# Seven products instead of eight for the pooling branch's first projection, with the weight sums made by GpSimd

## The chip, the cores and the metric

The kernel runs on one core of one Trainium2 chip. The metric is the device time of one execution in microseconds (us), and a kernel's time is the median of its runs. The engines are named as the profile names them: PE is TensorE, PEld its weight loads, DVE is VectorE, ACT is ScalarE, POOL is GpSimd and SP is SyncE, which here only issues DMAs.

## The reference

One layer of a hybrid encoder over 2048 positions of width 1024, in float32. The part that matters here:

```python
xn = rmsnorm(x, norm1_g[l])
z = xn @ w_in[l]
u_pool, zq, zf, zi, zo, zg = jnp.split(z, splits, axis=-1)
gates = jax.nn.sigmoid(zg + b_gate[l]).reshape(B, S, N_BRANCHES, D_MODEL)
ya = pool_mixer(u_pool, pool_w[l], pool_scale[l]) @ w_pa[l]
yb = hgrn2_mixer(zq, zf, zi, zo, lower_bounds[l], hgrn_norm_g[l]) @ w_pb[l]
merged = gates[:, :, 0] * ya + gates[:, :, 1] * yb
x = x + merged @ w_o[l]
x = x + conv_glu_ffn(rmsnorm(x, norm2_g[l]), w_up[l], conv_w[l], conv_b[l], w_down[l])
```

`pool_mixer` gives 512 channels, `w_pa` is 512 x 1024. The change concerns the product with `w_pa` alone.

## The kernel before

The sequence is worked in two halves of 1024 positions. Each half has two row blocks of 512 positions, called hf = 0 and 1 in the code. A half runs through these stages, one after another on PE: the projection `io`; 14 units of the input projection (named fr, gr and ur in the profile, for forget/query, gates and pooling input); `pa`, the projection of the pooled rows with `w_pa`; `pb`, the same for the HGRN branch; the output projection `wo`; the up-projection `up` and the down-projection `dn` of the feed-forward network.

Every float32 product is made of three matmuls: each operand is split into a high half (a cast on ACT, line 231 for weights and line 655 for rows) and a low half (a subtraction on DVE, lines 232 and 656), and high x high, high x low and low x high are added up in PSUM. All matmuls of the projections are issued on line 148.

All projections but `pa` and `pb` use a scheme with seven products instead of eight for a 2 x 2 block product (Winograd's form of Strassen's). A `Unit` holds two blocks of output channels for both row blocks. Its seven products, P1 to P7, come in the order P1, P6, P5, P7, P2, P4, P3 and take as their row operand the forms B11, T2, T1, T3, B21, T4 and B22; T1 to T4 are sums and differences of row blocks, and four of the seven weights are sums of weight blocks, s1 to s4. Three PSUM banks of a unit, X, Z and V, collect the products, and after most products DVE or ACT takes an intermediate result out. In the first half the weight sums of the input projection are made by POOL (line 443), partly in place in the raw weight tiles, and kept in DRAM for the second half.

`pa` and `pb` are plain. `branch` goes through eight tiles of 128 output channels in `M_ORDER`; for each tile and each row block a chain of 4 x 3 matmuls of 128x512 fills one bank, and one DVE instruction multiplies it by its gate (lines 1516 and 1518, output `ya` in pa). The gates come back from DRAM as tiles `gl`, asked for three channel tiles ahead.

Weights go through one `Stream` in the order of use: SP loads raw tiles (line 197) into a ring of 8, ACT and DVE split them into a ring of 6 `ops` tiles, and at most `LOOKAHEAD` = 4 tiles are made ahead of the one in use. Most other SBUF tiles come from one ring of 77 slots of 512 columns.

Side work runs in generator tasks, which are advanced one step after every six matmuls. Four of them matter here. `pa_task` starts with the last gate unit's first product, fetches the eight pooled tiles (`mx`, four for each row block, written to DRAM before by the pooling tasks) and splits them (`mxs`). Three runners carry the HGRN heads; the last of them end during pa. `halves_task` fetches and splits the HGRN outputs (`oT`, split to `oTs`) for pb; it starts in pa with the fifth of eight channel tiles (`O_AT`). `prepare` makes sums of later weights by DMA and pauses from the last gate unit to the end of pb. The order on each engine is set by a scheduler from the program's order and a time model, with a few dependencies written by hand.

Of the kernel before, what the change touches and what calls it, by code (L numbers as in the profile page):

```python
# [15 lines left out]
ALU = mybir.AluOpType  # L16
# [65 lines left out]
def tile_trunk(  # L82
# [26 lines left out]
    def slot(name, cols=TB, dt=F32):  # L109
        return slots.tile([P, cols], dt, tag="s", name=name, padded_shape=[P, 528])  # L110
# [32 lines left out]
    def join(task):  # L143
        while task.live:
            task.step()

    def mm(*args, **kw):
        count[1] = pe.matmul(*args, **kw)  # L148
        count[0] += 1
        if count[0] % MM_PER_TICK == 0:  # L150
            tick()
# [193 lines left out]
    def plan_one(key, src):  # L345
        r = stream.raw(src)
        stream.op(key, lambda nm, r=r: r.tile, [r])
# [44 lines left out]
    def plan_unit(key, src, kind, i, order, b0):  # L392
        mv, mg = proj_tiles(kind, i)
        if b0:
            unit = sums_of_unit(src, mv, mg, lambda p: lambda: kept["in", (kind, i), SUM_OF[p]])
        else:
            unit = weights_of_unit(src[mv], src[mg], (kind, i))
        for p in order:
            fn, raws = unit[p]()
            stream.op(key, fn, raws)  # L400

    def plan_mixer(b0):
        plan_io(b0)
        for kind, i in PROJ:
            if (kind, i) == ("u", 0):
                plan_one("pw", pool_wt)
            plan_unit("in", w_in_t, kind, i, ORDER, b0)
        for key, src in (("pa", w_pa_t), ("pb", w_pb_t)):
            for i in range(8):
                plan_one(key, src[i // 2][:, i % 2 * 512 : i % 2 * 512 + 512])  # L410
        plan_rows("wo", w_o, R_OUT, KD // 2)

    def proj_tiles(kind, i):
# [6 lines left out]
    def quarters(src_v, src_g):  # L420
        return [s[:, c * 512 : (c + 1) * 512] for s in (src_v, src_g) for c in range(2)]
# [8 lines left out]

        return {p: (lambda p=p: plan(p)) for p in ORDER}

    def weights_of_unit(src_v, src_g, unit):
        src = quarters(src_v, src_g)
        raws, made = {}, {}

        def raw(i):
            if i not in raws:
                raws[i] = stream.raw(src[i])
            return raws[i]  # L440

        def comb(key, t, x0, x1):
            pool.tensor_tensor(t, x0, x1, ALU.add)  # L443
            made[key] = t
            return t

        def plan(p):
            rs = [raw(i) for i in {"P1": (0,), "P6": (0, 2, 3), "P5": (2,), "P7": (0,),
                                   "P2": (1,), "P4": (3,), "P3": (1,)}[p]]

            def fn(nm):
                if p == "P6":
                    q0, q2, q3 = (r.tile for r in rs)
                    comb("s3", q0, q0, q2)
                    comb("s2", slot(f"{nm}s2"), q0, q3)
# [6 lines left out]
                keep(("in", unit, SUM_OF[p]), t)  # L462
                return t

            return fn, rs

        return {p: (lambda p=p: plan(p)) for p in ORDER}
# [181 lines left out]
    def split(src, name, on_pool=False):  # L649
        hi = slot(name + "h", TB, F32R)  # L650
        lo = slot(name + "l", TB, F32R)
        if on_pool:
            up = pool.tensor_scalar(hi, src, 1.0, 0.0, ALU.mult, ALU.add)
        else:
            up = act.copy(hi, src)
# [302 lines left out]
    def fetch(d, name, eng=sp):  # L958
        t = slot(name)
        eng.dma_start(t, d)  # L960
        return t
# [189 lines left out]
    def value(dst, a, ps):  # L1151
        if a is None:
            act.copy(dst, ps)
            return
        t, how = a
        if how == "from":
            return dve.tensor_tensor(dst, ps, t, ALU.subtract)  # L1157
        return dve.tensor_tensor(dst, t, ps, ALU.add if how == "add" else ALU.subtract)  # L1158

    class Unit:  # L1160
# [9 lines left out]

        def multiply(self, p, forms, late):
            xs = need(forms, FORM[p], late)
            self.forms = forms
            w = stream.get(self.key)
# [5 lines left out]
            for k in range(4):  # L1180
# [6 lines left out]
                mm(ps, wl, xh, start=False, stop=k == 3, skip_group_check=True)  # L1187
            stream.used(1)

        def after(self, p):  # L1190
            bk, t = self.bank, self.t
# [174 lines left out]
    def mixer(b0, forms, late):  # L1366
# [93 lines left out]
        def gate(s, m, hf):  # L1460
            if (s, m, hf) not in gates:
                gates[s, m, hf] = fetch(gd[s, m, hf], f"gl{b0 + hf}_{s}_{m}")
            return gates[s, m, hf]

        def pa_task():
            yield from halves_task(md, range(4), mixed, "mx", 2)
            for m in M_ORDER[:2]:
                for hf in range(2):
                    gate(0, m, hf)

        emits = {"fq": emit_fq, "u": emit_u, "g": emit_g}
        mixed, oT = {}, {}
# [41 lines left out]
        def gated(t, hf, g, ps):  # L1514
            if hf:
                dve.scalar_tensor_tensor(t, g, -1.0, ps, ALU.mult, ALU.mult)
            else:
                dve.tensor_tensor(t, g, ps, ALU.mult)

        def evac_a(m, hf, g, ps):  # L1520
            y[m, hf] = slot(f"ya{b0 + hf}_{m}")
            gated(y[m, hf], hf, g, ps)

        def evac_b(m, hf, g, ps):
            gated(g, hf, g, ps)
# [3 lines left out]
                two = {(h, r): y[k + r * (KD // 2), h] for h in range(2) for r in range(2)}  # L1529
                add_forms(two, yf, k, f"yf{b0}", eng=dve)  # L1530

        join(mtask)
        otask = []

        def start_o(n):
            if n == O_AT:
                otask.append(Task(halves_task(od, range(HEADS), oT, "oT", O_LAG)))

        branch("pa", 0, mixed, evac_a, start_o)
        while any(t.live for t in runners):  # L1540
            for t in runners:
                if t.live:
# [334 lines left out]
```

## Time and profile before

| | |
|---|---|
| median of 3 runs | 2521.32 us (2520.7 to 2521.7) |
| profiled execution | 2522.21 us |
| its span, first to last instruction | 2520.5 us |
| mean granted clock of TensorE | 0.998 |
| PE busy | 2506.8 us, 99% |
| DVE busy | 1943.3 us, 77% |
| ACT busy | 1196.0 us, 47% |
| POOL busy | 747.0 us, 30% |
| pa's matmuls, share of the chain that ended last | 4% |

The profile is that of one execution. Times within it count from its first instruction. In a row of a view that groups instructions, the line, engine, operation, output and inputs come first, then the count, the busy time in us, the mean of one instruction in ns, and the idle time of the engine just before with what ended it. A row of the view by stretches gives for each engine its busy time and instructions, then the granted clock, the DMA engines' busy share and GB/s.

### The profile page before, as it was taken

What the parts mean: (1) busy time and instruction counts of PE and PEld (TensorE: products, weight loads), DVE (VectorE), ACT (ScalarE), POOL (GpSimd) and SP (SyncE); (2) the same over time, 40 slices, a digit from 0 to 9 for tenths busy, and PEclk for the clock granted to TensorE, in tenths of its full rate; (3) what the DMA queues carried; (4) which work ended last, traced back from release to release, by engine and by line L of the source; (5) the groups of instructions that cost most, each with busy time, mean ns of one, the idle gap of its engine ahead of it and who ended that gap; (6) DMA issues with size and microseconds to landing.
All of it is one profiled execution on the core that took longest, in us unless ns stands there. A gap on an engine that the chain in (4) does not pass through costs nothing.

```text
span 2520.5 us, 35649 instructions
## 1 busy us (share of the span) xinstructions
PE 2506.8 (99%) x11508; PEld 2055.4 (82%) x11508; DVE 1943.3 (77%) x3476; ACT 1196.0 (47%) x2250; POOL 747.0 (30%) x1127
## 2 busy tenths in 40 slices
PE   9999999999999999999999999999999999999998
PEld 7888888888888888888788888888888888888887
DVE  7788877597998778885596778766979887778755
ACT  6534444235555445553554444442355555445534
POOL 4343452003344333551320202100033433325410
PEclk9999999999999999999999999999999999999999
DMA  8877787777888789897345343457344454447852
GB/s 271 271 201 223 212 218 226 251 204 244 207 253 240 223 224 246 265 364 233 114 155 155 105 134 109 142 158 236 124 155 120 153 150 138 149 135 247 319 165 98
DMA packets 252332, 493.76 MB, mean 196 GB/s; under 512 B 26544, under 2 KB 43056, under 8 KB 251824
## 3 DMA queue, kind: packets, MB, share of 16 engines
q1 hardware_dynamic: 184512, 313.60, 39.6%
q0 software_dynamic: 42656, 112.74, 17.6%
q10 hardware_dynamic: 24976, 65.13, 7.6%
q8 instruction: 91, 1.49, 0.3%
q14 instruction: 97, 0.79, 0.1%
HBM read 381.79 MB, written 187.17 MB: 226 GB/s over the span
## 4 chain that ended last, share of the span: by engine, by line
PE 98%; ACT 1%; POOL 0%; DVE 0%; DMA 0%; issue 0%; SPq 0%; POOLq 0%; DVEq 0%; ACTq 0%
PE dn_P L148 16%; PE up_Z L148 15%; PE up_X L148 10%; PE up_V L148 10%; PE wo_P L148 6%; PE gr_Z L148 5%; PE gr_V L148 4%; PE gr_X L148 4%; PE pa L148 4%; PE pb L148 4%; PE io_Z L148 3%; PE fr_Z L148 3%; PE fr_X L148 2%; PE io_V L148 2%; PE fr_V L148 2%; PE pl L1025 2%
## 5 line engine op out<-in xcount | busy, mean ns | idle before, releaser
L231 ACT CAST ops<-raw 128x512 fp32r<-128x512 f32 x786 | 485.4, 620 | 852.3 <-PE dn_P L148 180.2
L232 DVE TENSOR_TENSOR ops<-raw,ops 128x512 fp32r<-128x512 f32 x786 | 578.3, 738 | 226.1 <-ACT ops L231 219.8
L1613 DVE SCALAR_TENSOR_TENSOR e<-h,cols,e 128x512 f32<-128x512 f32 x176 | 143.1, 817 | 31.3 <-ACT e L1611 26.4
L1611 ACT ACTIVATE e<-h,cols 128x512 f32<-128x512 f32 x176 | 142.3, 815 | 25.0 <-DVE h L1158 18.3
L1616 DVE SCALAR_TENSOR_TENSOR e<-h,cols,e 128x512 f32<-128x512 f32 x176 | 133.9, 770 | 2.5
L960 POOL DMA_DIRECT2D g_P<-dg_P x154 | 84.0, 546 | 161.0 <-PE dn_P L148 110.8
L1268 POOL TENSOR_TENSOR gf_P<-e,e 128x512 f32<-128x512 f32 x44 | 61.1, 1390 | 149.6 <-DVE e L1622 96.1
L1268 POOL TENSOR_TENSOR gf_P<-gf_P,e 128x512 f32<-128x512 f32 x44 | 59.3, 1348 | 72.1 <-DVE e L1622 71.6
L1606 POOL COPY h<-h 128x2 f32<-128x2 f32 x88 | 40.2, 468 | 117.5 <-DVE h L1157 110.6
L1620 ACT ACTIVATE e<-e 128x512 f32<-128x512 f32 x88 | 55.6, 632 | 38.7 <-DVE e L1616 38.6
L1408 POOL TENSOR_TENSOR q<-q,qs 128x512 f32<-128x512 f32 x16 | 21.4, 1335 | 168.0 <-ACT qs L1407 168.0
L1608 POOL COPY hist<-h 128x2 f32<-128x2 f32 x88 | 35.5, 404 | 118.5 <-DVE h L1158 116.7
L443 POOL TENSOR_TENSOR raw<-raw,raw 128x512 f32<-128x512 f32 x28 | 38.9, 1390 | 102.0 <-DVE ops L232 101.0
L1158 DVE TENSOR_TENSOR h<-up_u,up_V 128x512 f32<-128x512 f32 x88 | 60.0, 682 | 10.3 <-PE up_V L148 9.9
L1243 DVE TENSOR_TENSOR x<-x,wo_P 128x512 f32<-128x512 f32 x88 | 56.0, 680 | 12.1 <-PE wo_P L148 11.9
L1445 ACT ACTIVATE gt<-gt,cols 128x512 f32<-128x512 f32 x48 | 34.8, 725 | 59.4 <-DVE gt L1158 42.5
L1243 DVE TENSOR_TENSOR ac<-ac,dn_P 128x512 f32<-128x512 f32 x72 | 47.0, 680 | 16.7 <-PE dn_P L148 16.6
L1010 POOL COPY qm<-q 128x64 f32<-128x64 f32 x64 | 27.1, 447 | 99.1 <-DVE q L1042 19.6
L1636 POOL DMA_DIRECT2D dg_P<-gf_P x88 | 50.8, 577 | 8.1 <-POOL gf_P L1268 7.4
L1193 ACT COPY up_e<-up_X 128x512 f32<-128x512 f32 x44 | 25.8, 587 | 57.7 <-PE up_X L148 52.6
L1606 POOL COPY h<-hist 128x2 f32<-128x2 f32 x88 | 45.0, 519 | 27.4 <-DVE m_T42l L656 27.4
L1025 PE MATMUL pl<-qm,k 128*128 128x192 f32 x256 | 50.2, 325 | 0.0
(1202 smaller groups left out, 8019.9 us busy)
## 6 DMA issues: line engine op xcount, KB each, us to landing
g_P<-dg_P POOLq DMA_DIRECT2D x154, 256.0 KB, 6.2
raw<-in_w_up_t SPq DMA_DIRECT2D x132, 256.0 KB, 3.3
raw<-in_w_in_t SPq DMA_DIRECT2D x98, 256.0 KB, 3.5
dg_P<-gf_P POOLq DMA_DIRECT2D x88, 256.0 KB, 4.0
dg_P<-e SPq DMA_DIRECT2D x66, 256.0 KB, 3.6
raw<-in_w_dn SPq DMA_DIRECT2D x66, 256.0 KB, 3.8
x<-in_x SPq DMA_DIRECT2D x64, 256.0 KB, 4.9
gd<-gt ACTq DMA_DIRECT2D x64, 256.0 KB, 3.5
```

Source lines behind the costliest of these rows:

```text
L148: count[1] = pe.matmul(*args, **kw)
L231: self.mark = act.copy(hi, v)
L232: low = self.low = dve.tensor_tensor(lo, v, f32(hi), ALU.subtract)
L960: eng.dma_start(t, d)
L1025: ins = pe.matmul(pa_[:, c * 192 : c * 192 + 192], ks[:, (i + c) * P : (i + c + 1) * P], mv[:, c].rearrange("p s x -> p (s x)"), start=Tru ...
L1158: return dve.tensor_tensor(dst, t, ps, ALU.add if how == "add" else ALU.subtract)
L1243: dve.tensor_tensor(t, t, ps[j], ALU.add if sg > 0 else ALU.subtract)
L1268: pin(eng.tensor_tensor(t, x0, x1, op))
L1606: pool.tensor_copy(h[:, 0:2], hist[:, mt] if hf == 0 else hs[s, 0][:, TB : TB + 2])
L1611: in_turn(act.activation(t, h[:, 2:], AF.Identity, bias=col(o_cb + mt), scale=col(o_cw + 4 * MF + mt)))
L1613: in_turn(second(dve.scalar_tensor_tensor(t, h[:, 1 : 1 + TB], col(o_cw + 2 * MF + mt), t, ALU.mult, ALU.add)))
L1616: dve.scalar_tensor_tensor(t, h[:, 0:TB], col(o_cw + mt), t, ALU.mult, ALU.add)
```

## The change

`pa` takes the form with seven products. The 1024 output channels are handled in two groups (d = 0, 1). A group has two `Unit`s (e = 0, 1), each with two channel tiles, i and i + 4. A weight tile of 512 columns now holds, for one product, two blocks of 128 rows for both units, so a product is 2 units x 2 x 3 matmuls, and there are 14 weight tiles instead of 8. Each group loads four raw quarters; POOL makes the sums s1 to s4 of them, s1, s3 and s4 in place in the raw tiles, s2 in a slot. Unlike those of the input projection they are not kept, and are made again in the second half.

`pa_task` fetches the same eight tiles, all before the first form, and makes the seven forms of two tiles each: t1, t2 and t4 on DVE, t3 on POOL, the negated B22 on ACT, and 14 splits. `emit_a` takes the results out: for block (0, 0) DVE multiplies PSUM by the gate; for the other three DVE combines PSUM with an intermediate result and POOL multiplies by the gate. Gates are asked for two products ahead of their use. The task for `oT` starts before the third product of the second group. The task of the forms need no longer be finished before pa starts; each product waits for its own form.

```diff
+        for d in range(2):
+            unit = weights_of_unit([w_pa_t[d][:, c * 512 : c * 512 + 512] for c in range(4)])
+            for p in ORDER:
+                fn, raws = unit[p]()
+                stream.op("pa", fn, raws)
+        for i in range(8):
+            plan_one("pb", w_pb_t[i // 2][:, i % 2 * 512 : i % 2 * 512 + 512])
...
         def pa_task():
-            yield from halves_task(md, range(4), mixed, "mx", 2)
-            for m in M_ORDER[:2]:
-                for hf in range(2):
-                    gate(0, m, hf)
+            t = {}
+            for hf, g in ((0, 0), (0, 1), (1, 0), (1, 2), (1, 1), (1, 3), (0, 2), (0, 3)):
+                while (b0 + hf, g) not in md:
+                    yield 1
+                t[hf, g] = fetch(md[b0 + hf, g], f"mx{b0 + hf}_{g}")
...
+            for j in range(2):
+                form("B11", j, t[0, j])
+                yield 1
+            t1, t2 = [], []
+            for j in range(2):
+                t1.append(minus("t1", j, t[1, j], t[0, j]))
+                t2.append(minus("t2", j, t[1, j + 2], t1[j]))
+                form("T2", j, t2[j])
+                yield 1
+            t3 = [minus("t3", j, t[1, j], t[1, j + 2], pool) for j in range(2)]
+            for j in range(2):
+                form("T1", j, t1[j])
+                yield 1
+            for j in range(2):
+                form("T3", j, t3[j])
+                yield 1
+            for j in range(2):
+                form("B21", j, t[0, j + 2])
+                t4 = minus("t4", j, t[0, j + 2], t2[j])
+                yield 1
+                form("T4", j, t4)
+                yield 1
+            for j in range(2):
+                x = slot(f"mf{b0}_b22{j}")
+                act.activation(x, t[1, j + 2], AF.Copy, scale=-1.0)
+                form("B22", j, x)
+                yield 1
...
+        def emit_a(i):
+            def emit(s, hf, a, ps):
+                m = i + KD // 2 * s
+                t = y[m, hf] = slot(f"ya{b0 + hf}_{m}")
+                g = gate(0, m, hf)
+                if a is None:
+                    dve.tensor_tensor(t, g, ps, ALU.mult)
+                    return
+                if not hf:
+                    value(t, a, ps)
+                elif s:
+                    dve.scalar_tensor_tensor(t, ps, -1.0, a[0], ALU.mult, ALU.subtract)
+                else:
+                    dve.tensor_tensor(t, ps, a[0], ALU.subtract)
+                pool.tensor_tensor(t, t, g, ALU.mult)
+            return emit
...
-        join(mtask)
         otask = []
-
-        def start_o(n):
-            if n == O_AT:
-                otask.append(Task(halves_task(od, range(HEADS), oT, "oT", O_LAG)))
-
-        branch("pa", 0, mixed, evac_a, start_o)
+        for d in range(2):
+            units = [Unit(f"pa{b0}_{2 * d + e}", "pa", emit_a(2 * d + e)) for e in range(2)]
+            for p in ORDER:
+                if (d, p) == (1, "P5"):
+                    otask.append(Task(halves_task(od, range(HEADS), oT, "oT", O_LAG)))
+                for s_, hf in {"P6": ((1, 1),), "P5": ((0, 0),), "P7": ((1, 0),),
+                               "P2": ((0, 1),)}.get(p, ()):
+                    for e in range(2):
+                        gate(0, 2 * d + e + KD // 2 * s_, hf)
+                while len(pf[FORM[p]]) < 2:
+                    mtask.step()
+                w = stream.get("pa")
+                for e in range(2):
+                    units[e].products(p, pf, pf[FORM[p]], w[:, :, e * 256 : e * 256 + 256])
+                    units[e].after(p)
+                stream.used(1)
```

More of the change, by code (lines that the diff above doesn't have):

```diff
@@ L396, in plan_unit @@
         else:
-            unit = weights_of_unit(src[mv], src[mg], (kind, i))
+            unit = weights_of_unit(quarters(src[mv], src[mg]), (kind, i))
         for p in order:
@@ L407, in plan_mixer @@
             plan_unit("in", w_in_t, kind, i, ORDER, b0)
-        for key, src in (("pa", w_pa_t), ("pb", w_pb_t)):
-            for i in range(8):
-                plan_one(key, src[i // 2][:, i % 2 * 512 : i % 2 * 512 + 512])
+        for d in range(2):
[5 more added lines that the diff above has]
+            plan_one("pb", w_pb_t[i // 2][:, i % 2 * 512 : i % 2 * 512 + 512])
         plan_rows("wo", w_o, R_OUT, KD // 2)
@@ L431, in sums_of_unit, with weights_of_unit @@
         return {p: (lambda p=p: plan(p)) for p in ORDER}
-    def weights_of_unit(src_v, src_g, unit):
-        src = quarters(src_v, src_g)
+    def weights_of_unit(src, unit=None):
         raws, made = {}, {}
@@ L461, in fn @@
                 t = made[SUM_OF[p]]
-                keep(("in", unit, SUM_OF[p]), t)
+                if unit is not None:
+                    keep(("in", unit, SUM_OF[p]), t)
                 return t
@@ L1172, in multiply, with products @@
             xs = need(forms, FORM[p], late)
+            self.products(p, forms, xs, stream.get(self.key))
+            stream.used(1)
+        def products(self, p, forms, xs, w):
             self.forms = forms
-            w = stream.get(self.key)
+            n = len(xs)
             kb = BANK[p]
@@ L1179, in multiply @@
             before = count[1]
-            for k in range(4):
+            for k in range(n):
                 wh, wl = w[:, 0, k * P : (k + 1) * P], w[:, 1, k * P : (k + 1) * P]
@@ L1186, in multiply @@
                 mm(ps, wh, xl, start=False, stop=False, skip_group_check=True)
-                mm(ps, wl, xh, start=False, stop=k == 3, skip_group_check=True)
-            stream.used(1)
+                mm(ps, wl, xh, start=False, stop=k == n - 1, skip_group_check=True)
         def after(self, p):
@@ L1463, in gate, with form, minus @@
             return gates[s, m, hf]
+        pf = {k: [] for k in ("B11", "B21", "B22", "T1", "T2", "T3", "T4")}
         def pa_task():
-            yield from halves_task(md, range(4), mixed, "mx", 2)
-            for m in M_ORDER[:2]:
-                for hf in range(2):
-                    gate(0, m, hf)
+            t = {}
[3 more added lines that the diff above has]
+                t[hf, g] = fetch(md[b0 + hf, g], f"mx{b0 + hf}_{g}")
+            def form(key, j, x):
+                pf[key].append(split(x, f"mf{b0}{key}{j}"))
+            def minus(key, j, x0, x1, eng=dve):
+                x = slot(f"mf{b0}_{key}{j}")
+                eng.tensor_tensor(x, x0, x1, ALU.subtract)
+                return x
+            for j in range(2):
[25 more added lines that the diff above has]
+                yield 1
         emits = {"fq": emit_fq, "u": emit_u, "g": emit_g}
-        mixed, oT = {}, {}
+        oT = {}
         for n, (kind, i) in enumerate(PROJ):
@@ L1518, in gated @@
                 dve.tensor_tensor(t, g, ps, ALU.mult)
-        def evac_a(m, hf, g, ps):
-            y[m, hf] = slot(f"ya{b0 + hf}_{m}")
-            gated(y[m, hf], hf, g, ps)
+        def emit_a(i):
[14 more added lines that the diff above has]
+            return emit
         def evac_b(m, hf, g, ps):
@@ L1530, in evac_b @@
                 add_forms(two, yf, k, f"yf{b0}", eng=dve)
-        join(mtask)
         otask = []
-        def start_o(n):
-            if n == O_AT:
-                otask.append(Task(halves_task(od, range(HEADS), oT, "oT", O_LAG)))
-        branch("pa", 0, mixed, evac_a, start_o)
+        for d in range(2):
[13 more added lines that the diff above has]
+                    units[e].after(p)
+                stream.used(1)
         while any(t.live for t in runners):
@@ L1847, in quarters_of, with fours_of @@
                         axis=2).reshape(-1, P, 2048)
+    def fours_of(w):
+        return w.reshape(2, 2, P, 2, 2, 2, P).transpose(4, 2, 3, 0, 5, 1, 6).reshape(2, P, 2048)
     def io_of(w):
@@ L1861 @@
         "pool_wt": a["pool_w"][0].transpose(1, 0, 2).reshape(P, 512),
-        "w_pa_t": pairs_of(a["w_pa"][0]),
+        "w_pa_t": fours_of(a["w_pa"][0]),
         "w_pb_t": pairs_of(a["w_pb"][0]),
```

## The prediction

> **What bounds the kernel now.** I read the page first: the busy times, and the chain that ended last.
>
> ```profile
> span 2520.5 us, 35649 instructions
> ...
> PE 2506.8 (99%) x11508; PEld 2055.4 (82%) x11508; DVE 1943.3 (77%) x3476; ACT 1196.0 (47%) x2250; POOL 747.0 (30%) x1127
> ...
> PE 98%; ACT 1%; POOL 0%; DVE 0%; DMA 0%; issue 0%; SPq 0%; POOLq 0%; DVEq 0%; ACTq 0%
> ```
>
> A busy PE alone proves little, since the ends of matmuls are modelled; that PE is 98% of the chain says more. Second, the list of waits, for PE alone:
>
> ```profile
> PE x_t L721 <- DVE x_xs L715: 3.7, 3, 2.0
> PE warm L681 <- POOL ident L562: 1.4, 1, 1.4
> PE io_Z L148 <- ACT ops L231: 0.5, 1, 0.5
> ```
>
> These are all of PE's waits, 5.6 us, and none is in the pooling projection. So a matmul that goes from a stage in the middle shortens the run by its own time, as long as nothing else becomes late there. Third, the chain in order of time, around the stage (pa) in the two halves of the sequence:
>
> ```profile
> 444.85 5.57 PE pa L148 x24
> ...
> 460.12 30.05 PE pa L148 x130
> 490.17 44.22 PE pb L148 x192
> ...
> 1711.66 28.98 PE pa L148 x125
> 1740.64 44.28 PE pb L148 x192
> ```
>
> The columns are start and length in us, then the count. One 128x512 matmul costs 30.05/130 = 0.231 us here, 28.98/125 = 0.232 in the second half. pa runs from 444.85 to 490.17, 45.3 us, with some transposes of the HGRN branch between.
>
> Fourth, the busy times by stage: the last gate unit before pa, pa, pb, the start of the output projection, and pa of the second half.
>
> ```profile
> core 0: us, PE busy (x) PEld busy (x) DVE busy (x) ACT busy (x) POOL busy (x), PEclk, DMA share, GB/s
> 421.00:445.00 24.00, 24.00 (x135) 20.58 (x134) 12.15 (x23) 10.77 (x26) 1.24 (x2) 1.00 0.65 201
> 445.00:490.00 45.00, 45.00 (x200) 36.51 (x199) 20.77 (x37) 13.05 (x29) 2.98 (x3) 1.00 0.81 251
> 490.00:534.00 44.00, 44.00 (x193) 35.85 (x192) 38.86 (x63) 7.58 (x13) 0.00 (x0) 1.00 0.71 240
> ```
> ```profile
> 534.00:560.00 26.00, 26.00 (x114) 21.11 (x113) 25.20 (x42) 16.14 (x29) 2.32 (x2) 1.00 0.66 181
> ```
> ```profile
> 1695.00:1740.00 45.00, 45.00 (x201) 36.46 (x200) 21.44 (x39) 13.08 (x28) 1.20 (x2) 1.00 0.68 217
> ```
>
> In pa DVE is busy 46% of the time and POOL hardly at all; in pb DVE is at 88%, and at the start of the output projection at 97% (25.20 of 26), and PE does not lose a tenth there. That is my measure of how full DVE may be before PE feels it.
>
> **The change part by part.** *TensorE.* Before, each half has 8 channel tiles x 2 row blocks x 4 x 3 = 192 matmuls. After, it has 2 groups x 7 products x 2 units x 2 x 3 = 168. Gone are 24 per half, 48 in all: 48 x 0.2315 = **11.1 us**. The matmul's shape stays the same, and there is one weight load less for each matmul less, so nothing is to be added on PE itself. A gain beyond 11.1 is excluded, because the stage has no wait of PE that could go. The durations of the work that comes in its place:
>
> ```profile
> L231 ACT CAST ops<-raw 128x512 fp32r<-128x512 f32 x786 | 485.4, 620 | 852.3 <-PE dn_P L148 180.2
> L443 POOL TENSOR_TENSOR raw<-raw,raw 128x512 f32<-128x512 f32 x28 | 38.9, 1390 | 102.0 <-DVE ops L232 101.0
> ...
> L1518 DVE TENSOR_TENSOR ya<-gl,pa 128x512 f32<-128x512 f32 x16 | 10.9, 682 | 4.8 <-PE pa L148 2.9 <-DMA gl<-gd 1.9
> L1268 DVE TENSOR_TENSOR yf_P<-ya,ya 128x512 f32<-128x512 f32 x16 | 10.8, 686 | 0.3
> ```
>
> *Forms of the pooled rows* (made by a task that starts at the last gate unit, as the splits before did). Before: 8 splits. After: 14 splits, and t1, t2, t4 on DVE (6 instructions), t3 on POOL (2), two negations on ACT. A split's low half on DVE is the same instruction as the weights' L232, which takes 687 ns around here (its row stands below). DVE gets 6 splits x 0.69 and 6 x 0.686 more, 8.3 us in a half.
> *Weights.* 14 tiles instead of 8: 6 casts on ACT (0.62) and 6 low halves on DVE (0.69, so 4.1 us). The sums are 4 on POOL for each group, 8 x 1.39 = 11.1 us in a half, and are made again in the second half.
> *Evacuation.* 16 products with the gate on DVE become six DVE instructions for each of 4 units, 24 x 0.682: 8 more, 5.5 us. ACT copies 4 times (at most a cast's 0.62), and POOL multiplies by the gate 12 times, 16.7 us.
> So each half adds 17.9 us to DVE, 30.6 to POOL (with t3) and about 11 to ACT, all beside PE. DMA moves what it moved: 8 fetches of mx, 16 of gates, 8 of weights, each of 256 KB.
>
> Does it fit? Before pa, 421 to 445: DVE has 12.15 us, of which 5 splits of mx are 3.5, so 8.7 of other work and 15.3 free. All forms together are 20 x 0.69 = 13.8 us, and just fit. In pa, now 45 - 5.6 = 39.4 us long: 20.77, less 3 splits (2.1) and 11 gate products (7.5), plus 24 x 0.682 = 16.4 and 6 x 0.69 = 4.1, is 31.7 us, 80%. POOL has some 24 us to do in the same time. What POOL does to DVE is seen in the up-projection:
>
> ```profile
> 640.00:1030.00 390.00, 390.00 (x1683) 315.83 (x1682) 329.11 (x464) 201.66 (x319) 156.18 (x228) 1.00 0.86 235
> ```
> ```profile
> L232 DVE TENSOR_TENSOR ops<-raw,ops 128x512 fp32r<-128x512 f32 x22 | 15.0, 687 | 10.1 <-ACT ops L231 10.1
> ```
> ```profile
> L232 DVE TENSOR_TENSOR ops<-raw,ops 128x512 fp32r<-128x512 f32 x142 | 110.0, 775 | 21.4 <-ACT ops L231 20.6 <-DMA raw<-in_w_dn 0.3 <-DMA raw<-in_w_up_t 0.2
> ...
> L1158 DVE TENSOR_TENSOR h<-up_u,up_V 128x512 f32<-128x512 f32 x41 | 28.0, 682 | 4.8 <-PE up_V L148 4.5
> ```
>
> The first row is the windows' row of 640 to 1030, where POOL is busy 40% and PE all the time; the next is L232 in 421 to 534, where POOL stands still, and the last two are of 640 to 1030. The split with two operands in SBUF takes 775 instead of 687 ns, while the one that reads PSUM stays at 682. In pa POOL is busier, 24 of 39.4 us or 60%, and 88 ns at 40% make some 130 at 60%; I add 0.09 to 0.2 us to each of some 25 such instructions: 2 to 5 us, hence 86 to 93% of DVE. That lies between pb's 88% and the 97% that cost PE nothing, so I put the evacuations and splits at nothing, with DVE's idle fifth as the cover. The Trainium skill says the same for a reason of its own: the page GPSIMD Engine Reference, section Specifications, has the SBUF interfaces of POOL shared with DVE and names DVE instructions with two SBUF inputs as those that contend. By that rule 24 PSUM readers are spared, as the 682 of L1158 bears out, and the bound from it is the first rival below.
>
> *Waits that are new on POOL:* a gate product waits for DVE and for its gate, and behind it stand the second group's sums s3, s2, s1, on which the cast of its P6 weight waits on ACT. The gates' landing, 415 to 492:
>
> ```profile
> DMA to landing us min/median/max: 4.1/5.9/11.2
> ```
>
> Weights are made four products, 11.1 us, ahead. Two sums, cast and low half take 2 x 1.39 + 0.62 + 0.69 = 4.1, the two gate products in front 2.8, and a gate asked for 5.6 us ahead is at most 5.6 late: between 0 and 4.1 + 2.8 + 5.6 - 11.1 = 1.4 us late, once in a half. I take nothing, from the median of 5.9.
>
> *A wait that moves:* the fetches and splits of the HGRN output (oT) that pb needs.
>
> ```profile
> L960 SPq DMA_DIRECT2D oT<-od x8: 319/382/384, 467.0 to 486.9; - x8
> L655 ACT CAST oTs_3h<-oT x2: 615/616/617, 479.6 to 491.4; 128x512 fp32r<-128x512 f32 x2
> ```
> ```profile
> 469.39 0.33 SPq L197 DMA_DIRECT2D raw<-in_w_o  x1
> ...
> 474.94 0.33 SPq L197 DMA_DIRECT2D raw<-in_w_o  x1
> ```
>
> Before, they began 23 us ahead of pb and ended at 491.4 + 0.6 + 0.7 = 492.7, 25.7 us later. Now they begin after 9 of 14 products, 5 x 2.78 = 13.9 us ahead. pa would end near 484.6 and the last of these splits is read by the third chain of pb, at 484.6 + 2 x 2.78 + 2.1 = 492.3. At the old pace the split would be ready at 470.7 + 25.7 = 496.4, 4.1 us late in each half. But the old pace was SP's: behind each weight load, 5.55 us apart as pa used one weight in two chains, the next fetches had to queue. Weights now go every 2.78 us, so the wait lies between 0 and 4.1. I take 0.75 in each half, near the lower end, 1.5 in all. A gain below zero from this part is excluded, since pb did not wait before.
>
> Sum: -11.1 + 1.5 = -9.6 us. The profiled execution took 2522.21 us (span 2520.5 and 1.7 around it) and would take 2512.6; it lies 0.9 above the median of the runs, 2521.32, which becomes **2511.7**.
>
> **The rivals.** *DVE is the bound for a part of the stage.* For: 13.8 us of forms against 15.3 free, and the 77 slots of the common buffer ring that the last gate unit frees 8 at a time; if half of the forms (6.9 us) slips into pa, DVE there has 31.7 + 6.9 + 2 to 5 = 41 to 44 us of work in 39.4. PE then waits 1.5 to 4.5 us in a half on top of the forecast, and the time is 2515 to 2521 (2511.7 + 3 to 9). Against: the 97% above. By the skill's rule on contention this is the case to come if POOL stretches the splits by more than the 0.2 us that I gave them.
>
> *Slower: the forms come too late.* The fetches of mx, the t's and the split halves take 46 slots where the splits of before took 24, while the last gate unit still holds most of its own forms. Two rows for it, from 445 to 467 and from 415 to 492:
>
> ```profile
> L1137 DVE SCALAR_TENSOR_TENSOR ot<-po,ro,z 128x128 f32<-128x128 f32 x8 | 2.2, 343 | 0.0
> ```
> ```profile
> L960 SPq DMA_DIRECT2D mx<-md x8: 372/430/1291, 421.0 to 448.4; - x8
> ```
>
> If only the first form (B11) is ready at 445, DVE has for the first group of seven: 18 x 0.69 = 12.4 of forms, 7 weights (4.8), 12 evacuations (8.2), HGRN's scaling of its output (2.2) and the last gate (0.7): 28.3 us where PE has 7 x 2.78 = 19.5. Each half then loses 8.8 us and gains 5.56, so the time is 2521.3 + 6.5 = 2527.8; a queue that stands that long on splits of 0.775 us instead of 0.69 adds 25 x 0.09 = 2.2 in a half, 2532 at most. It decides against the change from 5.6 us lost in a half, which is when about 13 of the 18 instructions slip. For it: the fetches of mx were issued up to 448.4 before. Against: they were spread by the task's own lag of two steps, and DVE idles half of 421 to 445.
>
> *The change does not save what it says* if matmuls were bound by something else than their number; the equal 0.231 in pa and 0.230 in pb (44.22/192) speaks against that, and I give it no chance of its own.
>
> **How the numbers follow.** Forecast 0.58: 2510.2 (nothing waits) to 2515 (oT late by 2.4 in each half, somewhat over half of its bound); its middle is weighted to the lower end as above. DVE as bound in part, with oT at its old pace or a part of the forms late: 0.22, 2515 to 2521.3. Forms too late as a whole: 0.20, 2526 to 2532 about the 2528 worked out. A measurement of this kernel tells 0.2%, about 5 us, from no change; that puts the limits at 2516.3 and 2526.3. Of the second case a quarter (0.06) lies below 2516.3. So faster 0.58 + 0.06 = 0.64, same 0.16, slower 0.20. The range starts at 2509.8, the full saving and half a microsecond of scatter, and goes to 2526, the foot of the slower case, so that 2 in 10 lie outside.
>
> **What would show it.** Right: 336 matmuls of pa instead of 384, at 0.231 us each; the chain from the first matmul of pa to the first of pb near 39.8 us in both halves; PE's waits still only at the start; DVE in pa at 80 to 93%, POOL near 60%. The step on oT is wrong if pb has a wait on oTs above 1.5 us, or none. The forecast is wrong if PE in pa waits for a mixer form or for weights (cast or POOL's sum), or if the split rows in pa go beyond 0.89 us; it is wrong in its ground if pa shrinks by 5.5 us in each half and another stage grows.

## The result, and the profile after

The changed kernel takes **2544.94 us** (median of 4 runs, 2540.95 to 2548.83) against 2521.51 (2520.7 to 2522.25) for the kernel before: a ratio of 1.0093, 95% interval 1.0075 to 1.011. It is 23 us slower where the prediction said 9.6 faster. The execution profiled took 2544.34 us.

The page of the changed kernel, its span, busy times and the engines' shares of the chain that ended last:

```profile
span 2542.6 us, 35725 instructions
...
PE 2505.1 (99%) x11460; PEld 2049.3 (81%) x11460; DVE 1989.2 (78%) x3528; ACT 1215.1 (48%) x2286; POOL 804.2 (32%) x1171
...
PE 91%; DVE 3%; DMA 2%; issue 1%; ACT 1%; POOL 1%; SPq 0%; ACTq 0%; POOLq 0%; DVEq 0%
```

48 matmuls are gone (11508 to 11460), and yet PE is busy about as long as before and has only 91% of the chain instead of 98%. Its waits, which before lay only at the start of the kernel (waited for, us in total, times, longest):

```profile
PE pb L148 <- ACT oTs_2h L659: 6.3, 2, 4.4
PE pb L148 <- ACT oTs_1h L659: 4.8, 2, 2.4
...
PE pa_Z L148 <- DVE pa_u L1202: 4.3, 2, 2.5
PE gr_Z L148 <- DVE gr_u L1206: 3.7, 2, 1.8
PE wo_P L148 <- ACT wo_P_3h L659: 2.5, 2, 1.3
```

Two kinds: the split HGRN output (oTs) for pb, and intermediate results (gr_u, pa_u) that DVE takes out of PSUM before PE may go on. The stretches of the prediction again, now for the changed kernel (busy us of PE, PEld, DVE, ACT, POOL, then granted clock):

```profile
421.00:445.00 24.00, 21.98 (x110) 18.27 (x110) 17.88 (x27) 10.35 (x26) 9.21 (x7) 0.93 0.52 175
445.00:490.00 45.00, 42.51 (x186) 33.95 (x184) 31.55 (x51) 20.18 (x42) 17.23 (x13) 0.96 0.52 172
490.00:534.00 44.00, 36.93 (x142) 28.50 (x143) 27.08 (x44) 8.30 (x14) 9.49 (x7) 0.92 0.71 211
```

PE stands for 2.0, 2.5 and 7.1 us, and the granted clock, 1.00 before in all three, is 0.92 to 0.96. DVE is less busy in the last stretch than before (27.08 us instead of 38.86): it isn't the bound there, it waits as well. The chain in order of time, around the passage from pa to pb (start, length):

```profile
480.74 5.92 DMA oT<-od
...
486.67 0.63 ACT oTs_0h L659
...
487.33 0.69 DVE oTs_0l L660
488.02 0.61 DVE ops L232
...
488.65 0.33 SPq L197
...
489.98 4.90 DMA oT<-od
...
494.90 0.63 ACT oTs_2h L659
...
495.57 2.80 PE pb L148 x6
498.37 1.94 PE pa_Z L148 x6
...
504.85 3.63 DMA oT<-od
...
509.90 39.66 PE pb L148 x164
```

Chain pieces of a transfer now stand where PE stood alone. They follow one another in a loop: a fetch of oT lands, ACT casts it, DVE splits it, DVE then splits the next weight, which frees a raw tile, SP loads the next raw weight into it, and only behind that load does SP issue the next fetch of oT. The scheduler has also put matmuls of pb ahead of the last ones of pa, and PE stands before one of these until 495.57. How late the fetches go out is seen in the timeline of SP (start, time, line, what):

```profile
480.74 0.43 SPq L964 DMA_DIRECT2D oT<-od  x1
481.26 2.96 SPq L197 DMA_DIRECT2D raw<-in_w_o  x2
484.28 0.46 SPq L964 DMA_DIRECT2D oT<-od  x1
...
489.98 0.42 SPq L964 DMA_DIRECT2D oT<-od  x1
...
504.85 0.43 SPq L964 DMA_DIRECT2D oT<-od  x1
...
507.63 0.91 SPq L964 DMA_DIRECT2D oT<-od  x2
```

Eight fetches take 27 us to be issued, from 480.7 to 508; before, they took 20, from 467.0 to 486.9.

### The profile page after: what moved, and what is told of

Same layout as the page of the kernel before. It is cut to its first block, busy times and chain, and to the rows that moved or that the text cites. A ratio compares the mean times of both kernels' runs of the same rounds, so it can differ in the third digit from the quotient of the medians.

```text
span 2542.6 us, 35725 instructions
## 1 busy us (share of the span) xinstructions
PE 2505.1 (99%) x11460; PEld 2049.3 (81%) x11460; DVE 1989.2 (78%) x3528; ACT 1215.1 (48%) x2286; POOL 804.2 (32%) x1171
## 3 DMA queue, kind: packets, MB, share of 16 engines
q8 instruction: 91, 1.49, 0.2%
## 4 chain that ended last, share of the span: by engine, by line
PE 91%; DVE 3%; DMA 2%; issue 1%; ACT 1%; POOL 1%; SPq 0%; ACTq 0%; POOLq 0%; DVEq 0%
PE dn_P L148 16%; PE up_Z L148 14%; PE up_X L148 10%; PE up_V L148 10%; PE gr_Z L148 5%; PE wo_P L148 5%; PE gr_X L148 3%; PE gr_V L148 3%; PE io_Z L148 3%; PE fr_Z L148 3%; PE pb L148 2%; PE io_V L148 2%; PE fr_V L148 2%; PE fr_X L148 2%; PE pl L1029 2%; PE ur_Z L148 1%
## 5 line engine op out<-in xcount | busy, mean ns | idle before, releaser
L232 DVE TENSOR_TENSOR ops<-raw,ops 128x512 fp32r<-128x512 f32 x794 | 590.5, 747 | 233.8 <-ACT ops L231 228.9
L446 POOL TENSOR_TENSOR raw<-raw,raw 128x512 f32<-128x512 f32 x36 | 51.2, 1423 | 150.5 <-DVE ops L232 136.5
L1580 POOL TENSOR_TENSOR ya<-ya,gl 128x512 f32<-128x512 f32 x24 | 34.2, 1441 | 73.7 <-DVE ya L1161 28.6
```

The costliest lines, as they stand in the source:

```text
L232: low = self.low = dve.tensor_tensor(lo, v, f32(hi), ALU.subtract)
```

## The experiments

Every kernel ran beside the kernel before, whose median was 2521.3 to 2521.9 each time. Ratios are to it, with the 95% interval.

**e1_before_168: the premise by itself.** The kernel before, with 168 matmuls of pa in each half instead of 192: it leaves out the fourth of the four channel groups for the second row block, so a part of that sum is missing. Nothing else is changed.

```diff
-                        [xs[hf, k] for k in range(4)])
+                        [xs[hf, k] for k in range(3 if key == "pa" and hf else 4)])
```

> The kernel before with the pooling projection cut to 168 matmuls in each half: for the second row block the fourth of four channel groups is left out, so its part of the sum is missing. Nothing else is changed. If 48 matmuls off PE are worth their own time (0.231 us each), the time is 2521.5 - 11.1 = 2510.4, and the fault lies in the work that comes in their place. If pa were bound by something else than PE, the time would stay within 3 us of 2521.5.

Measured: 2508.46 us, ratio 0.9948 (0.9933 to 0.9963), 12.8 us less. Its chain passes to pb at 484.44 instead of 490.17, and without a wait:

```profile
460.23 24.21 PE pa L148 x105
484.44 44.32 PE pb L148 x192
```

So the saving is there, in full. What the changed kernel lost, 34.5 us (the 23.4 that it is slower, and the 11.1 that it saved), was lost by the rest of the change.

**e2_pin_pb: the order of PE.** Each chain of pb is held behind the matmul issued before it in the program, so that none overtakes pa.

```diff
     def chain_t(ps, w_of, xs, start=True, stop=True):
+        before = count[1]
...
+            if k == 0:
+                behind(count[1], before)
```

> The changed kernel with one thing more: each chain of pb is held in order behind the matmul ahead of it, so that PE finishes pa before it starts pb (in the changed kernel the first 24 matmuls of pb stand ahead of the last 24 of pa). Theory A (the seam: pb's rows oT come late, and PE, DVE and SP each wait in order behind them): part of the 11.5 us lost between the last product before the interleaving and the end of pb in the first half goes; I expect 2530 to 2540, since oT still starts late. Theory B (the forms of the pooled rows and POOL's sums slow DVE ahead of and in the first group of pa): hardly a change, 2541 to 2547.

Measured: 2541.64, 1.0081 (1.0066 to 1.0096), by the time a case of theory B. But the waits of pb went, and another one took their place:

```profile
PE pa_Z L148 <- DVE pa_u L1209: 14.8, 3, 7.6
```

This is the same delay at a new place, as theory A has it. In the changed kernel already, pa_u stood behind a split of oT in DVE's own queue; its DVE timeline says how long (idle time before, and what ended it, in brackets):

```profile
495.55 0.69 DVE L660 TENSOR_TENSOR oTs_2l<-oT,oTs_2h 128x512 fp32r<-128x512 f32 x1 [5.03 <-ACT oTs_2h L659]
496.16 0.68 DVE L1206 TENSOR_TENSOR pa_u<-pa_Z,pa_e 128x512 f32<-128x512 f32 x1
```

Whichever of the two PE waits for, it waits for a late oT.

**e3_pin_early: the same work begun earlier.** The pin, and the task of oT started with the first group's P3 instead of the second group's P5.

```diff
-                if (d, p) == (1, "P5"):
+                if (d, p) == (0, "P3"):
```

> As the kernel with pb held behind pa, and the task that fetches and splits oT starts with the last product of the first group instead of the third of the second, three products or 8.4 us earlier. Theory A: pb has no more wait on oTs, both halves win back most of what the seam lost (11.5 and some 7 us), 2523 to 2528. Theory B: 2538 to 2545, the loss stays ahead of pb.

Measured: 2541.84, 1.0078 (1.0062 to 1.0095): no gain, and again in theory B's range, though the loss lies where theory A puts it. PE waits 21.2 us in four pieces for pa_u, one product earlier. The fetches now go out from 468.1 to 485.1, as early as in the kernel before. What an earlier start doesn't change is DVE's order, in which pa_u stands behind a split that waits for its fetch:

```profile
485.97 0.69 DVE L660 TENSOR_TENSOR oTs_0l<-oT,oTs_0h 128x512 fp32r<-128x512 f32 x1 [3.19 <-ACT oTs_0h L659]
486.58 0.68 DVE L1205 TENSOR_TENSOR pa_u<-pa_e,pa_Z 128x512 f32<-128x512 f32 x1
```

SP stands in line as well. This is its longest item of waits in 440 to 505:

```profile
SPq L197 <- DVE ops L232: 49.6, 12, 13.3
```

For 49.6 of these 65 us SP stands at a raw weight load whose tile DVE has not yet freed, and a fetch of oT stands behind it. By itself this sum says little: it is 54.7 us in the changed kernel, 29.4 in the kernel before, and still 42.8 in e9 below, where no wait on oT is left.

**e5_pin_actq: another queue.** The pin, and the fetches of oT issued by ACT instead of SP, at their place in the changed kernel.

```diff
-                    t = fetch(src[b0 + hf, g], f"{name}{b0 + hf}_{g}")
+                    t = fetch(src[b0 + hf, g], f"{name}{b0 + hf}_{g}", eng)
```

> The changed kernel with pb held behind pa and with the eight fetches of oT issued on ACT's queue instead of SP's, at the same place in the program. Theory A1 (a fetch of oT stands on SP behind a raw load that waits for a split on DVE, and that split stands behind a split of oT that waits for the fetch before; each fetch so costs a round of several us): the longest wait of PE on pa_u, 7.6 us with SP's queue, falls below 4, and the time is 2528 to 2536 instead of 2541.6. Theory A2 (the fetches are late only because the task starts late): hardly a change, 2539 to 2543.

Measured: 2545.57, 1.0099 (1.0084 to 1.0114), slower than both theories had it. So raw loads on SP aren't the cause by themselves. The ACT timeline shows what delays the fetches here:

```profile
478.68 0.36 ACTq L967 DMA_DIRECT2D oT<-od  x1
...
482.36 0.62 ACT L659 CAST oTs_0h<-oT 128x512 fp32r<-128x512 f32 x1 [0.30 <-DMA oT<-od]
482.37 0.33 ACTq L967 DMA_DIRECT2D oT<-od  x1
...
486.54 0.62 ACT L659 CAST oTs_1h<-oT 128x512 fp32r<-128x512 f32 x1 [1.68 <-DMA oT<-od]
486.55 0.33 ACTq L967 DMA_DIRECT2D oT<-od  x1
...
491.35 0.62 ACT L659 CAST oTs_2h<-oT 128x512 fp32r<-128x512 f32 x1 [3.67 <-DMA oT<-od]
491.35 0.33 ACTq L967 DMA_DIRECT2D oT<-od  x1
```

A cast waits for its transfer, and the next fetch is issued only behind that cast. So the first transfers run one at a time, three of them 3.7, 4.2 and 4.8 us from issue to cast, and there are eight.

**e6_pin_prefetch, e9_prefetch_sp, e10_prefetch_only: all eight asked for ahead.** A task of its own issues the eight fetches from the first group's P3 on, and another splits them later. In e6 the fetches go on ACT's queue, with the pin. e9 is e6 with SP's queue, e10 is e6 without the pin.

```diff
+                if (d, p) == (0, "P3"):
+                    ftask = Task(fetch_task())
                 if (d, p) == (1, "P5"):
-                    otask.append(Task(halves_task(od, range(HEADS), oT, "oT", O_LAG)))
+                    join(ftask)
+                    otask.append(Task(split_task()))
```

> As the kernel with pb held behind pa and the fetches on ACT's queue, and all eight fetches are issued at the last product of the first group, ahead of the splits, which start as in the changed kernel. Theory A1 and A2 both: no split of oT on DVE waits for a DMA any more, PE's waits in the second group go, and what is left is the loss ahead of it (g7 and first group, some 8 us in the first half and 4 in the second, clock included): 2519 to 2527. If a loss stays in the second group, DVE's own load there is the cause, 2528 to 2538.

> As e6_pin_prefetch (2521.0), but the eight fetches of the HGRN output are issued on SP's queue, among the loads of raw weight tiles, instead of on ACT's. Theory A3 (what cost the time was that a fetch stood behind the splits of the fetch before it, in whichever in-order queue; all eight asked for ahead, any queue will do): 2519 to 2523, no wait of PE on oTs or behind their splits. Rival (SP's queue itself is the cause, because raw loads that wait for a free tile stand ahead of the fetches): the fetches trickle out over the last products of pa again, and PE waits 8 to 15 us at the seams: 2530 to 2542.

> As e6_pin_prefetch, but without the pin: PE's order at the seam is left to the scheduler again. Theory A3 (the fetches alone are the cause; the interleaved order of pa and pb was a way of filling the time that the scheduler foresaw): 2519 to 2523. Rival (the interleaving costs by itself, since pb's matmuls of the interleaved part need oT early): PE again waits on oTs at both seams, 5 to 10 us in all, 2526 to 2535.

Measured: e6 2521.01, 0.9999 (0.999 to 1.0009); e9 2520.15, 0.9995 (0.9986 to 1.0004); e10 2521.00, 0.9996 (0.9986 to 1.0005). Neither the queue nor the pin matters: with the eight fetches ahead, 24 us of the changed kernel's loss are back. In e6 the fetches are issued within 4.4 us (its rows of oT, first and last start), and no wait on oT is left:

```profile
L967 ACTq DMA_DIRECT2D oT<-od x8: 326/442/750, 470.5 to 474.9; - x8
```
```profile
PE pa_Z L148 <- DVE pa_u L1205: 4.3, 2, 2.5
PE gr_Z L148 <- DVE gr_u L1209: 3.7, 2, 1.8
```

In e9 SP issued six in a row at 467.73, where the program of the changed kernel has a cast and a split between any two. In e10 PE still runs matmuls of pb ahead of the last ones of pa (from 485.15 on) and waits for none of them, so the interleaved order is not a cause. These kernels both issue the fetches together and issue them earlier. That the earlier start alone gains nothing is shown by e3; all eight together at the late start was not run.

**e4_dma_sums: the weight sums off POOL.** The changed kernel with the sums of pa's weights made once by DMA in DRAM, as those of the later stages are, instead of by POOL in the raw tiles.

```diff
-        todo = [sums[name].make(g) for name in ("wo", "up", "dn")
+        todo = [sums[name].make(g) for name in ("pa", "wo", "up", "dn")
```

> The changed kernel with the weight sums of pa made by DMA in DRAM, once, ahead of all others, as those of the output projection are; pa then loads 14 raw tiles in each half instead of 8, and POOL makes no sums for it. Theory B, with POOL's sums as what doubles DVE's forms before pa (1.7 to 1.8 us instead of 0.69): the waits on gr_u and pa_u go, 2530 to 2537. Theory A: they cost 3 to 8 us at most, and the waits of pb on oTs stay at 10 us or more: 2537 to 2543.

Measured: 2548.31, 1.0106 (1.009 to 1.0121). The waits on gr_u and pa_u fell from 8.0 to 4.1 us, and the up-projection of the first half began 9 us earlier. But the sums for the down-projection, which the same task makes, now came late (waits on dn_P of 6.3 us), and the waits on oT stayed. The time lies above both ranges, because the run mixes two effects. The next runs part them.

**e7_no_pool_sums, e12_lag_only, e13_dma_sums_lag7: the sums and the pause, parted.** All three stand on e6. e13 has the sums by DMA. e12 has the pause between such DMA sums cut from 7 steps to 6 (`SUM_LAG = 6`), with the sums of pa left on POOL. e7 has both.

> As the kernel with all eight fetches ahead, and POOL makes no weight sums for pa: they are made once by DMA in DRAM (with a lag of 6 instead of 7 steps between the DMA sums, so that those of the down-projection are not late). Theory B for what is left: POOL's sums double the first forms on DVE in the last gate unit, so the waits on gr_u and pa_u shrink from 3.7 and 4 us to under 2 each, and the time is 3 to 7 us below that of the kernel with POOL's sums. If DVE's number of instructions is the cause, not POOL, less than 2 us.

> As e6_pin_prefetch (2521.0), with the one other edit that e7_no_pool_sums had beside the sums by DMA: the pause between the sums made by DMA is 6 steps instead of 7. It is the control for e7. Theory (e7 gained its 6 us from POOL's sums leaving the first forms on DVE alone): no change from e6_pin_prefetch, 2519.5 to 2523, with the waits of PE on gr_u and pa_u still near 8 us. Rival (the other pace moves transfers and tasks in a way that gains by itself): 2515 to 2518.

> The cell that is missing beside e6_pin_prefetch (sums by POOL, pause 7: 2521.0), e7_no_pool_sums (sums by DMA, pause 6: 2514.7) and e12_lag_only (sums by POOL, pause 6: 2527.5): sums of pa by DMA, pause of 7 steps. Theory (the sums on POOL cost the first forms 6 us or more; the pause does nothing good by itself, and 6 was only needed so that the down-projection's sums are not late): 2513 to 2519, with 3 to 4 us of PE's waits on gr_u and pa_u left and up to 6 us of waits in the down-projection. Rival (it was the pause and the sums only together that gained): 2520 to 2524.

| | sums by POOL | sums by DMA |
|---|---|---|
| pause 7 | e6: 2521.01 | e13: 2524.65, 1.0012 (1.0002 to 1.0021) |
| pause 6 | e12: 2527.52, 1.0021 (1.0012 to 1.0031) | e7: 2514.73, 0.9976 (0.9967 to 0.9985) |

**e7 is faster than the kernel before, by 6.8 us**, and e6 to e7 is as expected; both controls, e12 and e13, missed what I expected of them, and by the times alone the two edits don't add up. In the stages around pa the effect of the sums can be read apart. First e6, then e7, busy time of PE in each stretch first:

```profile
420.00:450.00 30.00, 28.17 (x144) 23.66 (x143) 22.99 (x35) 15.04 (x40) 10.88 (x8) 0.94 0.50 171
450.00:500.00 50.00, 47.51 (x203) 38.27 (x202) 41.72 (x65) 19.83 (x37) 26.81 (x19) 0.97 0.75 254
```
```profile
420.00:450.00 30.00, 29.34 (x156) 24.82 (x155) 23.34 (x43) 17.75 (x45) 5.40 (x6) 1.00 0.65 226
450.00:500.00 50.00, 49.04 (x216) 39.48 (x216) 41.91 (x66) 19.47 (x35) 19.67 (x14) 1.00 0.89 292
```

With 1680 to 1800 of the second half, PE stands for 8.0 us in these stages in e6 and 7.5 in e12 (sums on POOL), and for 3.3 in e7 and 3.3 in e13 (sums by DMA), whatever the pause. The clock is 0.94 and 0.97 in e6, and 1.00 in both stretches in e7, e13 and e12. The other differences lie in other stages. e13 lost 7.95 us in 1030 to 1400, the down-projection, at sums that were late (first row below); e12 lost 3.5 us at 140 to 220, in the input projection (second row, PE busy 76.54 of 80, where e6 has 80.00), and 1.3 more in 640 to 1030:

```profile
PE dn_P L148 <- ACT dn_P_6h L663: 5.1, 1, 5.1
```
```profile
140.00:220.00 80.00, 76.54 (x395) 63.68 (x394) 65.81 (x155) 33.57 (x77) 38.22 (x43) 1.00 0.81 212
```

So the theory holds for the sums: on POOL they cost PE 4 to 5 us of standing in the stages around pa. The slower clock came with these waits in e6's profiled execution, not in e12's. At 140 to 220 PE waits for a gr_u in every run with a pause of 6 (2.4 us in e12, 0.3 in e7, and 1.6 and 1.8 in e11 and e8 below), and in no run with 7. Why, and why so much less in e7, was not followed up.

**e8_calm and e11_t3_dve: the rest of the forms.** e7 with t3 on DVE instead of POOL (e11), and with t3 on DVE just before its use and a slower pace of the first forms (e8).

```diff
-            t3 = [minus("t3", j, t[1, j], t[1, j + 2], pool) for j in range(2)]
+            t3 = [minus("t3", j, t[1, j], t[1, j + 2]) for j in range(2)]
```

> As the kernel without POOL's sums, with the forms T2 and T1 two steps apart instead of one and t3 made by DVE when it is needed instead of by POOL ahead: fewer instructions of forms stand ahead of the gate unit's own evacuations. If these are what still delays gr_u, its waits go and the time is 2510 to 2518; if the forms are then late for pa's own products, PE waits for mf forms instead, 2518 to 2526.

> As e7_no_pool_sums (2514.7), but t3 is made on DVE instead of POOL, so that POOL has nothing but gate products in the stage; e8_calm had this together with a slower pace of the forms and took 2517.2. Theory (what is left are DVE's first forms doubled by t3 on POOL): the waits on gr_u and pa_u of 3.6 us go below 1.5, 2511.5 to 2513.5. Rival (the two more DVE instructions delay the evacuations as much as they spare): 2514.5 to 2517.5, and then e8_calm's loss came from here rather than from the pace.

Measured: e8 2517.19, 0.9984 (0.9975 to 0.9994); e11 2517.68, 0.9982 (0.9972 to 0.9992). Their medians lie 2.5 and 3.0 us above e7's, though the intervals overlap. In e11 PE waits 3.6 us on gr_u where e7 has 1.7. Only a part of that belongs to t3: the two waits in the last gate units are 0.97 us each, where e7 has 0.66 and 0.73. The third, 1.6 us, lies at 214 in the input projection, with the pause of 6. So t3 on DVE gains nothing in its own stage, and loses some 0.6 us there; the rest of the loss lies elsewhere and is not explained. e7 stays the best version.

## Why the prediction was wrong, point by point

*The saving on TensorE was right.* 11.1 us were forecast; e1, which leaves out as many matmuls, gave 12.8 with an interval that holds 11.1. In e7 the sum nearly closes as well: 11.1 saved, less the 3.6 us that PE still waits on gr_u and pa_u, makes 7.5, and 6.8 were measured.

*The step that failed first is the wait for oT.* It was put at 0 to 4.1 us a half and taken at 0.75, 1.5 in all. Measured by its removal (e6, and e10, which has no other edit, against the changed kernel) it is **24 us**. The bound rested on the sentence that "the old pace was SP's", and that the fetches would come faster as weights went faster. The pace was that of fetch, cast and split one after another in in-order queues, as e5 shows without SP. The raw loads ahead of a fetch did not go faster either. They wait for DVE's weight splits (54.7 us in 440 to 505 of the changed kernel, 29.4 in the kernel before), and these stand behind DVE's splits of oT, which wait for the fetch. Nor was the start at 470.7 as worked out; the first fetch was issued at 480.74, in a stage that had begun 3.7 us late and in which PE had stood 2.5 us for pa_u and then run at a lower clock. Only the arrival of the last split was priced, not that pa_u and the weights stand behind each split on DVE.

*The second step that failed is that the forms "just fit".* 13.8 us of forms against 15.3 us free counted each at 0.69, and contention with POOL was added only inside pa, at 0.09 to 0.2 us each. But the sums of pa's first weights and t3 fall into the last gate unit, where the first forms are. The timelines of the changed kernel there, DVE and then POOL:

```profile
427.51 1.82 DVE L660 TENSOR_TENSOR mf0B110l<-mx,mf0B110h 128x512 fp32r<-128x512 f32 x1
429.25 1.75 DVE L660 TENSOR_TENSOR mf0B111l<-mx,mf0B111h 128x512 fp32r<-128x512 f32 x1
430.93 0.67 DVE L1202 TENSOR_TENSOR gr_u<-gr_e,gr_Z 128x512 f32<-128x512 f32 x1
...
440.30 0.68 DVE L1206 TENSOR_TENSOR gr_u<-gr_Z,gr_e 128x512 f32<-128x512 f32 x1
```
```profile
427.49 2.97 POOL L446 TENSOR_TENSOR raw<-raw,raw 128x512 f32<-128x512 f32 x2 [7.87 <-DMA mx<-md]
430.42 3.42 POOL L1486 TENSOR_TENSOR mf_t<-mx,mx 128x512 f32<-128x512 f32 x2
```

Each of the two splits took 1.1 us more, five to twelve times the price; in e7, without the sums on POOL, the same two take 0.69 and 0.68. The gr_u for which PE waits 1.8 us is the one at 440.30. It stands behind these splits, the t's and the next forms, the last three of them (0.69, 0.68 and 0.68 us) right ahead of it. The prediction weighed only how full DVE would be, with a busy share of 97% as harmless. The changed kernel lost PE time at 74% (17.88 of 24): what counts is whose result stands behind what in DVE's order. This step cost 6.3 us by the times of e6 and e7, which differ in the pause too; 4 to 5 us of PE standing in these stages are what the pause leaves untouched. Inside pa the price by the average nearly held: the weight splits there took 0.90 us in the first half and 0.84 in the second, where 0.78 to 0.89 was forecast.

*Right:* POOL's sums made no direct wait of PE; none of PE's waits in pa is on a weight. The evacuations and splits within pa fit in DVE's time: once the two causes are gone DVE is busy 41.91 of the 50 us from 450 to 500 in e7, 84%, within the 80 to 93% forecast.

*The rivals.* None had this mechanism. "The forms come too late" was the nearest, and its price of 2526 to 2532 lay too low as well: its place, the last gate unit and the first group, is where the smaller loss was, and it said nothing of pb. The rival that took DVE as the bound in part gave 2515 to 2521.3. The check named for oT (a wait above 1.5 us in pb) found the failed step: 6.3 and 4.8 us on oTs_2h and oTs_1h.

*What is left.* 33.2 us lie between forecast and measurement. In the order in which they were taken away, these are 24 for oT, 6.3 for the sums on POOL with the pause, and 3.0 from e7 to 2511.7. Of these, 2.1 are waits still there (3.6, less the 1.5 that the forecast had for oT).

## What to carry to other kernels

A fetch that feeds the next stage is issued for all its tiles before the first is consumed; alternated with its consumer in an in-order queue, a fetch starts only when the tile before it has been used, and any other result behind that consumer is late too. When a bounded wait is priced, price also what stands behind the waiting instruction on every engine of the loop. A transfer of work to an idle engine is priced where the work will fall, not where the stage is that it belongs to.

## What the runs showed of the hardware that was not expected

*DVE beside POOL.* DVE's subtraction of two SBUF operands, 0.69 us alone, took 1.0 to 1.8 us (five of them, 427 to 436) where it lay beside POOL instructions of 1.5 to 1.7 us, while gr_u, which reads PSUM, took 0.67 in the same stretch. The prediction took 0.09 to 0.2 us from an average over 390 us, where POOL was busy 40%. The Trainium skill, SBUF — State Buffer, section "SBUF: two separate sides", says that such a DVE instruction and a POOL instruction take an exclusive lock for the whole instruction and the loser waits it out. This trace agrees in the main: the 1.1 us added to the two splits are some three quarters of one POOL instruction of 1.49 us, where a wait for the whole of it would have added 1.49.

*The clock after short gaps.* Before the first row below PE stood for 1.83 us for gr_u, until 441.04 (chain of the changed kernel):

```profile
441.04 4.61 PE gr_Z L148 x12
445.65 2.77 PE gr_V L148 x12
```

Twelve matmuls took 4.61 us and the next twelve 2.77, so here a wait of 1.8 us cost another 1.8 in slower matmuls; the granted clock of 439 to 445 is 0.72. In e7, with a wait of 0.7, it is 1.00 there. The Trainium skill, TensorE: Matmul & The Clock Gate, Part 1, section "What's actually happening", gives an idle window of some 3.4 us for the throttled clock. Here it fell after a wait shorter than that, and the measurement decides. But it doesn't always fall: the same wait of 1.83 us in the second half of the same execution, until 1704.51, was followed by matmuls at full pace, with a granted clock of 1.00 until 1709.12. In the stages around pa (400 to 580 and 1660 to 1810), in the profiled executions of the changed kernel and of e2 to e13, none of 23 waits of 0.6 to 1.5 us was followed by a run of slow matmuls, 12 of 27 waits of about 1.8 us were, 9 of 13 of 2.3 to 2.6 us, and all 8 longer ones. What decides in between was not found. So in this kernel a wait of 1.8 us may cost up to twice its length.
